# A two-layer float32 trunk on one core: opening, norms' rows, the place of float32 values, and the order of halves' chunks changed

## The chip, the cores and the metric

The kernel runs on one core of one Trainium2 chip. Its time is the device time of one launch in microseconds, the median of three runs. A profile is one further execution, recorded by the hardware profiler. The engines are named as in the profile: PE (TensorE matmul) and PEld (its weight loads), DVE (VectorE), ACT (ScalarE), POOL (GpSimd), SP (SyncE, which issues most transfers).

## What is computed

The reference runs two decoder layers on 256 tokens of width 2048, all in float32. The first layer mixes tokens by softmax attention with a forget gate (16 heads of 128), the second by a mixture of three dilated windows (8 heads, values of 256). Each mixer is followed by an MLP with squared ReLU, and each sub-layer stands behind an RMSNorm and adds into one residual stream.

```python
def rms_norm(x, g):
    y = xf * lax.rsqrt(jnp.mean(xf * xf, axis=-1, keepdims=True) + EPS)
    return (y * g).astype(x.dtype)

def sq_relu_mlp(h, w_up, w_down):
    a = jax.nn.relu(h @ w_up)
    return (a * a) @ w_down

def reference(x, ...):
    for i in range(DEPTH):                      # DEPTH = 2
        h = rms_norm(x, mix_norm_g[i])
        mix = fox_attention(...) if i % 2 == 0 else dilated_attention(...)
        x = x + mix
        h = rms_norm(x, mlp_norm_g[i])
        x = x + sq_relu_mlp(h, mlp_w_up[i], mlp_w_down[i])   # 2048 -> 8192 -> 2048
    return x
```

## The kernel before

**Products.** The whole program is a row of products of 256 tokens with weight matrices that are read once from memory. A weight block of 256 rows and 512 columns (`raw`, 524 KB) is loaded by SP, and split into a high part (`wh`, a cast by ACT) and a low part (`wl`, the difference, by DVE). The activations are split likewise (`hT` for normed inputs, `aTh`/`aTl` for the MLP's inner values, `oT` for attention outputs). A product then takes three matmuls for each 128 rows of the weight (a step, named k) and each of the two token blocks t: high x high, high x low and low x high (lines 421 to 423). One step is therefore six matmuls of 512 columns. A unit is one split weight block, two steps. Five raw blocks and five split units are held at a time, so that loads and splits run ahead of PE; a split of a later unit and the load of a still later one are issued after each unit (`split`, `next_load`, lines 343 and 387).

**Order.** Nothing is left to a scheduler. The program is traced as the main row of products, and every other piece of work (norms, attention heads, gates, the turning of activations) is a generator, a job. After each step the main row calls `jobs.tick()`, which resumes every job whose time has come: `yield 4` in a job means "go on four steps later", `yield key` means "go on when that key is done". The method `pin` fixes that order on each engine. So a number in a `yield` says between which products a piece of work stands in each engine's queue; every engine works through its queue in order.

**Opening.** PE begins with idle matmuls on a tile of zeros (`wake`, line 153). SP loads x in four pieces of 512 columns (`load_x`; the first in three parts), the norm gains and the first weight blocks. The first block comes in two halves (lines 1109 and 1119), the others in one transfer each (line 338). The mixers' norm gains come as rows, `g_mix`, and are turned into columns by a PE transpose and a DVE copy (`gain_rows`, `gain_columns`). For each 128 columns of x PE transposes two blocks into `ptx` (line 564), ACT makes the high part of `hT` and DVE the low one (lines 566 and 567). `row_blocks` splits a unit in halves of 128 rows, so that a step can begin on the first half. The job `opening` issues the first splits, and the job `more_constants` loads the forget gate's weights and two more sets of gains, `g_qk` (8 rows) and `g_mlp` (32 rows), each with a transpose of its own.

**Attention.** A head's scores (`scores`) are one float32 product for the first token block (which the profile shows as two matmuls, a pair) and three split ones for the second. After the softmax its rows are turned through memory (`p_turned`), split (`p_split`, tile pT), and multiplied with the values (`pv`): three split matmuls of 256 columns and one float32 product. `fox_head` and `dil_head` are the jobs of one head; `at` and the yields in them place scores and values. `gate_chain` makes the forget gate's running sums.

**MLP.** Each MLP works on four blocks (b) of 2048 inner columns, each of four chunks (n) of 512. In block 0 all four chunks are plain products. In blocks 1 to 3 the chunks 0 to 2 are made by a Strassen scheme with seven half-sized products for each slice of 256 weight rows (`slice_steps`, tiles halves_n); its weights need sums of quarters (`sum_quarters`), which cost DVE more than a plain unit does. These slices are woven between the units of the down product of block b-1 and of chunk 3 of block b. The lists `BETWEEN` and, for b = 1 (period one), `FIRST_BETWEEN` say after which of the period's 40 units each of the 24 slices (8 for each chunk) stands. A finished chunk goes through `halves_chain` (or `up_chain`, if plain) and `turn_up`: DVE transposes 32x32 squares, SP writes them to memory in four transfers for each token block and reads them back in one, ACT and DVE split the result into `aTh` and `aTl` (lines 1009 and 1011).

Of the kernel before, what the change touches and what calls it, by code (L numbers as in the profile page):

```python
# [46 lines left out]
SUM_TAGS = ("kh3", "kl3", "kh4", "kl4", "kh5", "kl5", "q0", "q1", "q2", "qkw0", "qkw1", "qkw2", "vh", "vl", "pT", "t1")  # L47

BETWEEN = (0, 1, 3, 4, 7, 9, 10, 11, 15, 16, 17, 18, 19, 20, 21, 22, 26, 27, 28, 29, 31, 33, 34, 35)
FIRST_BETWEEN = (0, 1, 2, 6, 8, 9, 10, 11, 15, 16, 17, 19, 20, 21, 22, 23, 27, 28, 30, 31, 33, 34, 36, 37)  # L50


class Jobs:
# [48 lines left out]
def trunk(ctx: ExitStack, tc, x, fox_w_in, fox_b_f, fox_q_gain, fox_k_gain, fox_w_out, dil_w_in,  # L102
# [50 lines left out]
    def wake(times):  # L153
        for _ in range(times):
            nc.tensor.matmul(spare, zeros[:, 0:P], zeros, start=True, stop=True)

    wake(9)


    gain = const.tile([P, 4 * KC + 8], F32, name="gain")  # L160
    MLP_G, FOX_G, DIL_G = 2 * KC, 4 * KC, 4 * KC + 2

    def gain_rows(name, sources):
        rows = work.tile([2 * KC, P], F32, tag="s", name=name, bufs=S_BUFS)
        at = 0
        for src in sources:
            nc.sync.dma_start(rows[at:at + src.shape[0], :], src)
            at += src.shape[0]
        return rows[0:at, :]
# [25 lines left out]
    def more_constants():  # L195
        yield 5
        wf = work.tile([P, KC, FH], F32, tag="t2", name="wf")
        nc.sync.dma_start(wf, fox_w_in[0][:, 3 * D:3 * D + FH].rearrange("(c p) n -> p c n", p=P))
        nc.sync.dma_start(bf, fox_b_f.to_broadcast([P, FH]))
        qk_rows = gain_rows("g_qk", [fox_q_gain, fox_k_gain, dil_q_gain[0], dil_k_gain[0]])  # L200
        mlp_rows = gain_rows("g_mlp", [mlp_norm_g.rearrange(per_chunk, p=P)])
        di = distances()
        yield 9
        nc.scalar.copy(wfs[:, :, 0:FH], wf)
        nc.vector.tensor_sub(wfs[:, :, FH:2 * FH], wf, wfs[:, :, 0:FH].bitcast(F32))
        jobs.done.add("wf")
        yield 1
        gain_columns("g_qk", qk_rows, FOX_G)
        for c in (FOX_G, DIL_G, DIL_G + 1, DIL_G + 2):
            nc.vector.tensor_scalar_mul(gain[:, c:c + 1], gain[:, c:c + 1], SCALE)  # L210
        yield 1
        gain_columns("g_mlp", mlp_rows, MLP_G)
        yield 1
        mask = work.tile([P, 3 * P], F32, tag="t0", name="mask")
        nc.vector.tensor_copy(mask, di)
        nc.vector.tensor_scalar(mask, mask, 0.0, None, ALU.is_ge)
        nc.vector.tensor_scalar(mask, mask, BIG, -BIG, ALU.mult, ALU.add)
        tables["mask"] = mask
        jobs.done.add("mask")
# [108 lines left out]
    def load():  # L328
        i = state["raw"]
        if i >= len(plan):  # L330
            return
        w, r, cols = plan[i]
        t = wpool.tile([P, RAW_SUB, NC], F32, tag="raw", name=f"raw{i}", bufs=RAW_BUFS)
        at = 0
        for c, width in cols:
            src = w[r:r + RAW_SUB * P, c:c + width].rearrange("(c p) n -> p c n", p=P)
            hold(t)
            nc.sync.dma_start(t[:, :, at:at + width], src)
            at += width
        raws.append(t)  # L340
        state["raw"] += 1
# [328 lines left out]
    def by_token(po):  # L670
        return po[:, 0:S].rearrange("p (n b) -> p b n", b=2)

    def pv(pt_sb, vt, cols, o_hi, o_lo, name, apart):
        for i, c in enumerate(cols):
            if i:
                yield 1
            po = ps_sc.tile([P, 512], F32, tag="sc", name=f"po_{name}_{i}")
            whole, v_hi, v_lo = vt
            p_hi, p_lo, p_whole = pt_sb
            for v, p, first in ((v_hi, p_hi, True), (v_hi, p_lo, False), (v_lo, p_hi, False)):  # L680
                nc.tensor.matmul(po[:, 0:S], v[:, c:c + P], p.rearrange("p (b n) -> p n b", b=2), start=first, stop=False)
            nc.tensor.matmul(by_token(po)[:, 1], whole[:, c:c + P], p_whole, start=False, stop=True)
            hi, lo = (o.rearrange("p (b n) -> p b n", b=2) for o in (o_hi[i], o_lo[i]))
            nc.scalar.copy(hi, by_token(po))
            yield apart
            nc.vector.tensor_sub(lo, by_token(po), hi.bitcast(F32))
# [60 lines left out]
    def gate_chain(tag, pf):  # L747
        yield (tag, "rstd")
        tri = work.tile([P, P], F32, tag="s", name="tri", bufs=S_BUFS)
        nc.gpsimd.memset(tri, 1.0)  # L750
        nc.gpsimd.affine_select(out=tri, in_=tri, compare_op=ALU.is_ge, fill=0.0, base=0,
                                pattern=[[1, P]], channel_multiplier=-1)
        ones = work.tile([P, P], F32, tag="s", name="ones", bufs=S_BUFS)
        nc.gpsimd.memset(ones, 1.0)
        f = work.tile([2 * FH, S], F32, tag="s", name="g_f", bufs=S_BUFS)
        nc.vector.tensor_copy(f, pf[:, 0:S])
        nc.vector.tensor_add(f, f, pf[:, S:2 * S])
        yield 3
        pft = ps_sc.tile([P, NT, 2 * FH], F32, tag="sc", name="pft")
        for t in range(NT):  # L760
            nc.tensor.transpose(pft[:, t, :], f[:, t * P:(t + 1) * P], ident[:2 * FH, :2 * FH])
        z = small.tile([P, NT, FH], F32, tag="g_z", name="g_z", bufs=1)
        for t in range(NT):
            r = rstd[tag][:, t:t + 1]
            nc.vector.scalar_tensor_tensor(z[:, t, :], pft[:, t, 0:FH], r, bf, ALU.mult, ALU.add)
            nc.vector.scalar_tensor_tensor(z[:, t, :], pft[:, t, FH:2 * FH], r, z[:, t, :], ALU.mult, ALU.add)

        neg = small.tile([P, NT, FH], F32, tag="g_n", name="g_n", bufs=1)
        nc.vector.tensor_scalar(neg, z, -1.0, None, ALU.mult)
        nc.vector.tensor_tensor(neg, neg, z, ALU.min)  # L770
        e = small.tile([P, NT, FH], F32, tag="g_e", name="g_e", bufs=1)
        nc.scalar.activation(e, neg, AF.Exp)
        yield 1
        u = small.tile([P, NT, FH], F32, tag="g_u", name="g_u", bufs=1)
        nc.vector.tensor_scalar(u, e, 2.0, None, ALU.add)
        nc.vector.reciprocal(u, u)
        nc.vector.tensor_mul(u, e, u)
        u2 = small.tile([P, NT, FH], F32, tag="g_u2", name="g_u2", bufs=1)
        nc.vector.tensor_mul(u2, u, u)
        s = small.tile([P, NT, FH], F32, tag="g_s", name="g_s", bufs=1)  # L780
        nc.vector.tensor_scalar(s, u2, 1.0 / 19.0, None, ALU.mult)
        for odd in (17, 15, 13, 11, 9, 7, 5, 3):
            nc.vector.scalar_tensor_tensor(s, s, 1.0 / odd, u2, ALU.add, ALU.mult)
        nc.vector.scalar_tensor_tensor(s, s, 1.0, u, ALU.add, ALU.mult)
        nc.vector.tensor_scalar(z, z, 0.0, None, ALU.min)
        lf = small.tile([P, NT, FH], F32, tag="g_lf", name="g_lf", bufs=1)
        nc.vector.scalar_tensor_tensor(lf, s, -2.0, z, ALU.mult, ALU.add)
        yield 10
        pc = ps_sc.tile([P, NT, FH], F32, tag="sc", name="pc")
        nc.tensor.matmul(pc[:, 0, :], tri, lf[:, 0, :], start=True, stop=True)  # L790
        nc.tensor.matmul(pc[:, 1, :], ones, lf[:, 0, :], start=True, stop=False)
        nc.tensor.matmul(pc[:, 1, :], tri, lf[:, 1, :], start=False, stop=True)
        nc.vector.tensor_copy(c_q, pc)
        yield 4
        pct = ps_sc.tile([FH, S], F32, tag="sc", name="pct")
        for t in range(NT):
            nc.tensor.transpose(pct[:, t * P:(t + 1) * P], c_q[:, t, :], ident)
        ct = work.tile([FH, 3 * P], F32, tag="s", name="g_ct", bufs=S_BUFS)
        nc.vector.tensor_scalar(ct[:, P:], pct, -1.0, None, ALU.mult)
        nc.vector.tensor_copy(ct[:, 0:P], ct[:, P:2 * P])  # L800
        move(negc, ct)
        jobs.done.add("gate")

    def fox_head(j, hh, qT, kT, vt):
        h = 4 * j + hh
        at = ((2, 7, 12, 16) if j == 3 else (3, 8, 18, 22))[hh]
        yield ("fq", j)
        yield "gate"
        yield "mask"
# [44 lines left out]
    def dil_head(q4, i, qTs, kTs, vt):  # L854
# [30 lines left out]
        turned = yield from p_turned(p, f"d{h}", 6 if q4 == 3 else 10)  # L885
        yield ("dv", q4)
        pt_sb = yield from p_split(turned, f"d{h}")
        yield 2 if q4 == 3 else 4
        if ("d", q4) not in oT:
            oT["d", q4] = tuple(  # L890
                act.tile([P, 4, S], F32R, tag=f"aT{x}", name=f"oTd{x}_{h}", bufs=KC // 4) for x in "hl")
# [234 lines left out]
        what()  # L1126

    gain_columns("g_mix", mix_rows, 0)
    wake(1)
    row_blocks = [slice(i, i + 1) for i in range(W_SUB)]  # L1130
    split(())
    split_part(0, row_blocks[0])
    jobs.spawn(first(0))
    split_part(0, row_blocks[1])
    next_load()
    load_x(3)
    del issued["paced"]
    issued["opening"] = True

    def opening():  # L1140
        yield 1
        split(row_blocks)
        yield 2
        split(row_blocks)
        yield 1
# [73 lines left out]
```

## Time and profile before

| | us |
|---|---|
| median of 3 runs | 2110.7 |
| lowest and highest run | 2109.43, 2110.99 |
| the profiled execution | 2110.77 |
| its span, first to last instruction | 2109.1 |

The page lists for each engine the busy time, its share of the span and the number of instructions; then the chain of work that ended last. A timeline row is: start in us from the span's start, busy us, engine (with q: its sequencer, which issues transfers), line, operation, out<-in by the program's names, shapes, count, and in brackets the idle time of that engine just before, with what ended it. A row of a window has the stretch, its length, the busy us and counts of PE, PEld, DVE, ACT and POOL, the granted clock of PE, the share of the DMA engines and GB/s. A matmul's end is modelled, so the distance between two starts tells more than the shown duration.

### The profile page before, as it was taken

How to read it: one execution, taken by the hardware profiler on the slowest of the kernel's cores; microseconds unless marked ns; L12 is line 12 of the kernel's file. 1: busy time of each engine (PE TensorE's matmuls, PEld its weight loads, DVE VectorE, ACT ScalarE, POOL GpSimd, SP SyncE). 2: the span in 40 equal slices, each digit the busy share in tenths (PEclk: the TensorE clock that was granted, in tenths of full speed). 3: DMA queues.
4: the chain of work that ended last, by engine and by line, in shares of the span. 5: the costliest groups of instructions: out<-in, count | busy, mean ns of one | idle time of the engine just before them, and what ended most of it. 6: DMA issues, size and time to landing. Idle time of an engine off the chain costs nothing.

```text
span 2109.1 us, 32200 instructions
## 1 busy us (share of the span) xinstructions
PE 2100.2 (100%) x11375; PEld 1881.1 (89%) x11375; DVE 1748.1 (83%) x2548; ACT 1288.6 (61%) x1869; POOL 139.9 (7%) x160
## 2 busy tenths in 40 slices
PE   9999999999999999999999999999999999999999
PEld 7888888889998999998888888888899999999988
DVE  6888876799999998988668777767899989999974
ACT  6565654766666666664656565645656666666652
POOL 2000000001001001000010010000001101101100
PEclk9999999999999999999999999999999999999999
DMA  7889877878878878887877776867878878878884
GB/s 244 259 260 266 255 245 215 285 255 230 269 214 250 274 231 251 259 261 244 269 240 228 247 236 213 265 210 242 275 225 251 258 236 251 251 258 245 249 265 150
DMA packets 374993, 518.26 MB, mean 246 GB/s; under 512 B 43096, under 2 KB 176560, under 8 KB 374832
## 3 DMA queue, kind: packets, MB, share of 16 engines
q1 hardware_dynamic: 360592, 503.23, 75.5%
q0 software_dynamic: 13824, 12.59, 3.9%
q8 instruction: 89, 1.46, 0.3%
q10 hardware_dynamic: 416, 0.39, 0.1%
q14 instruction: 72, 0.59, 0.1%
HBM read 463.12 MB, written 40.39 MB: 239 GB/s over the span
## 4 chain that ended last, share of the span: by engine, by line
PE 93%; DVE 3%; ACT 1%; DMA 1%; issue 1%; SPq 0%; ACTq 0%; DVEq 0%
PE acc L422 25%; PE acc L421 25%; PE acc L423 25%; PE halves_n L1061 5%; PE halves_n L1060 5%; PE halves_n L1059 5%; ACT wh L370 1%; DVE wl L371 1%; PE halves_n L1057 0%; DMA raw<-in_dil_w_in_dram 0%; PE sc_d L733 0%; DMA raw<-in_fox_w_in_dram 0%; DVE quarters L380 0%; PE sc_f L733 0%; DMA turned_n1a<-blocks_n1a 0%
## 5 line engine op out<-in xcount | busy, mean ns | idle before, releaser
L371 DVE TENSOR_TENSOR wl<-raw,wh 128x1024 fp32r<-128x1024 f32 (+1 forms) x659 | 790.6, 1213 | 263.4 <-ACT wh L370 254.2
L370 ACT CAST wh<-raw 128x1024 fp32r<-128x1024 f32 (+1 forms) x659 | 680.5, 1043 | 426.6 <-PE acc L423 332.0
L421 PE MATMUL acc<-wh,hT_n 128*128 128x512 f32 x1344 | 512.7, 381 | 1.1 <-ACT wh L370 0.8
L422 PE MATMUL acc<-wl,hT_n 128*128 128x512 f32 x1344 | 509.6, 379 | 0.2 <-DVE wl L371 0.2
L423 PE MATMUL acc<-wh,hT_n 128*128 128x512 f32 x1344 | 509.5, 379 | 0.0
L370 ACT CAST wh<-quarters 128x1024 fp32r<-128x1024 f32 x144 | 151.5, 1052 | 229.7 <-DVE quarters L384 195.0
L423 PEld LDWEIGHTS acc<-wh,hT_n 128*128 128x128 f32 x1344 | 254.0, 189 | 36.2 <-DVE hT_n L567 0.2
L421 PEld LDWEIGHTS acc<-wh,hT_n 128*128 128x128 f32 x1344 | 254.3, 189 | 35.4 <-ACT wh L370 1.2
L422 PEld LDWEIGHTS acc<-wl,hT_n 128*128 128x128 f32 x1344 | 254.3, 189 | 34.4 <-DVE wl L371 0.8
L371 DVE TENSOR_TENSOR wl<-quarters,wh 128x1024 fp32r<-128x1024 f32 x144 | 175.8, 1221 | 36.7 <-ACT wh L370 36.6
L422 PE MATMUL acc<-wl,aTh_n1a 128*128 128x512 f32 x512 | 194.2, 379 | 0.6 <-DVE wl L371 0.6
L421 PE MATMUL acc<-wh,aTh_n1a 128*128 128x512 f32 x512 | 194.2, 379 | 0.0
L423 PE MATMUL acc<-wh,aTl_n1a 128*128 128x512 f32 x512 | 194.0, 379 | 0.0
L422 PE MATMUL acc<-wl,aTh_n3a 128*128 128x512 f32 x480 | 182.0, 379 | 0.6 <-DVE wl L371 0.6
L421 PE MATMUL acc<-wh,aTh_n3a 128*128 128x512 f32 x480 | 182.1, 379 | 0.0
L423 PE MATMUL acc<-wh,aTl_n3a 128*128 128x512 f32 x480 | 181.9, 379 | 0.0
L1061 PE MATMUL halves_n<-wh,sums_n 128*128 128x256 f32 x576 | 158.4, 275 | 0.0
L1060 PE MATMUL halves_n<-wl,sums_n 128*128 128x256 f32 x576 | 158.4, 275 | 0.0
L1059 PE MATMUL halves_n<-wh,sums_n 128*128 128x256 f32 x558 | 153.4, 275 | 0.0
L366 ACT CAST wh<-raw 128x768 fp32r<-128x768 f32 x144 | 119.9, 833 | 53.5 <-PE acc L423 29.3
L368 DVE TENSOR_TENSOR wl<-raw,wh 128x768 fp32r<-128x768 f32 x144 | 137.0, 952 | 2.0 <-ACT wh L366 2.0
L1060 PE MATMUL halves_n<-wl,hT_n 128*128 128x256 f32 x432 | 119.0, 276 | 0.3 <-DVE wl L371 0.3
(664 smaller groups left out, 3374.4 us busy)
## 6 DMA issues: line engine op xcount, KB each, us to landing
raw<-in_mlp_w_up_dram SPq DMA_DIRECT2D x256, 512.0 KB, 5.0
raw<-in_mlp_w_down_dram SPq DMA_DIRECT2D x256, 512.0 KB, 4.9
raw<-in_dil_w_in_dram SPq DMA_DIRECT2D x192, 256.0 KB, 3.5
raw<-in_fox_w_in_dram SPq DMA_DIRECT2D x95, 512.0 KB, 4.9
raw<-in_fox_w_out_dram SPq DMA_DIRECT2D x32, 512.0 KB, 4.8
raw<-in_dil_w_in_dram SPq DMA_DIRECT2D x32, 512.0 KB, 4.6
raw<-in_dil_w_out_dram SPq DMA_DIRECT2D x32, 512.0 KB, 4.3
x<-y_n POOLq DMA_DIRECT2D x96, 128.0 KB, 6.6
```

The costliest lines, as they stand in the source:

```text
L366: nc.scalar.copy(flat_hi, flat)
L368: nc.vector.tensor_sub(flat_lo, flat, flat_hi.bitcast(F32))
L370: nc.scalar.copy(hi[:, part, :], raw[:, part, :])
L371: nc.vector.tensor_sub(lo[:, part, :], raw[:, part, :], hi[:, part, :].bitcast(F32))
L421: nc.tensor.matmul(acc[t], ah[:, tok], hi, start=first, stop=False)
L422: nc.tensor.matmul(acc[t], ah[:, tok], lo, start=False, stop=False)
L423: nc.tensor.matmul(acc[t], al[:, tok], hi, start=False, stop=last)
L1059: nc.tensor.matmul(to, ah, hi, start=pr == 0 and i == 3, stop=False)
L1060: nc.tensor.matmul(to, ah, lo, start=False, stop=False)
L1061: nc.tensor.matmul(to, al, hi, start=False, stop=pr == KC // 2 - 1 and i > 2)
```

## The change

The idle matmuls become 8 (9 + 1 before). The second weight block is loaded in two transfers of 128 rows, and its first half is split before the opening job starts. The gains of `g_qk` and `g_mlp` are gathered in one tile of 40 rows and turned by one transpose; the columns of the gain table move accordingly. In `pv` the float32 product of the values stands third instead of last. One step more is put ahead of the gate's last transposes, of the scores of the first head of the last group of four (j == 3), and of the dilated heads' value products (for the first three groups). In period one 13 of the 24 slices move to earlier units.

```diff
-FIRST_BETWEEN = (0, 1, 2, 6, 8, 9, 10, 11, 15, 16, 17, 19, 20, 21, 22, 23, 27, 28, 30, 31, 33, 34, 36, 37)
+FIRST_BETWEEN = (0, 1, 2, 6, 8, 9, 10, 11, 15, 16, 17, 18, 19, 20, 21, 22, 26, 27, 28, 30, 31, 33, 34, 35)
...
-    wake(9)
+    wake(8)
...
-    MLP_G, FOX_G, DIL_G = 2 * KC, 4 * KC, 4 * KC + 2
+    MLP_G, FOX_G, DIL_G = 2 * KC + 8, 2 * KC, 2 * KC + 2
...
-        rows = work.tile([2 * KC, P], F32, tag="s", name=name, bufs=S_BUFS)
+        rows = work.tile([2 * KC + 8, P], F32, tag="s", name=name, bufs=S_BUFS)
...
-        qk_rows = gain_rows("g_qk", [fox_q_gain, fox_k_gain, dil_q_gain[0], dil_k_gain[0]])
-        mlp_rows = gain_rows("g_mlp", [mlp_norm_g.rearrange(per_chunk, p=P)])
+        rows = gain_rows("g_rest", [fox_q_gain, fox_k_gain, dil_q_gain[0], dil_k_gain[0],
+                                    mlp_norm_g.rearrange(per_chunk, p=P)])
...
-        gain_columns("g_qk", qk_rows, FOX_G)
+        gain_columns("g_rest", rows, FOX_G)
...
-        yield 1
-        gain_columns("g_mlp", mlp_rows, MLP_G)
...
             hold(t)
-            nc.sync.dma_start(t[:, :, at:at + width], src)
+            for rows in [slice(k, k + 1) for k in range(RAW_SUB)] if i == 1 else [slice(0, RAW_SUB)]:
+                nc.sync.dma_start(t[:, rows, at:at + width], src[:, rows])
...
-            for v, p, first in ((v_hi, p_hi, True), (v_hi, p_lo, False), (v_lo, p_hi, False)):
-                nc.tensor.matmul(po[:, 0:S], v[:, c:c + P], p.rearrange("p (b n) -> p n b", b=2), start=first, stop=False)
-            nc.tensor.matmul(by_token(po)[:, 1], whole[:, c:c + P], p_whole, start=False, stop=True)
+            for v, p, at in ((v_hi, p_hi, 0), (v_hi, p_lo, 1), (v_lo, p_hi, 2)):
+                if at == 2:
+                    nc.tensor.matmul(by_token(po)[:, 1], whole[:, c:c + P], p_whole, start=False, stop=False)
+                nc.tensor.matmul(po[:, 0:S], v[:, c:c + P], p.rearrange("p (b n) -> p n b", b=2), start=at == 0, stop=at == 2)
...
         nc.vector.tensor_copy(c_q, pc)
-        yield 4
+        yield 5
...
-        at = ((2, 7, 12, 16) if j == 3 else (3, 8, 18, 22))[hh]
+        at = ((3, 7, 12, 16) if j == 3 else (3, 8, 18, 22))[hh]
...
         pt_sb = yield from p_split(turned, f"d{h}")
-        yield 2 if q4 == 3 else 4
+        yield 2 if q4 == 3 else 5
...
     gain_columns("g_mix", mix_rows, 0)
-    wake(1)
...
     split_part(0, row_blocks[1])
     next_load()
+    split(())
+    split_part(1, row_blocks[0])
     load_x(3)
...
     def opening():
         yield 1
-        split(row_blocks)
+        split_part(1, row_blocks[1])
+        next_load()
         yield 2
```

## The prediction

> **What bounds the kernel now.** I read the page first, then the waits of the tensor engine (PE), then the timelines at the places these waits name.
>
> ```profile
> PE 2100.2 (100%) x11375; PEld 1881.1 (89%) x11375; DVE 1748.1 (83%) x2548; ACT 1288.6 (61%) x1869; POOL 139.9 (7%) x160
> PE 93%; DVE 3%; ACT 1%; DMA 1%; issue 1%; SPq 0%; ACTq 0%; DVEq 0%
> ```
>
> The span is 2109.1 us and PE is busy in all but 9 of them, 93% of the chain that ended last is PE. No edit removes a product, so the change can only give back what PE loses between products. In the waits, a row ends in total us, number of waits, longest:
>
> ```profile
> PE acc L422 <- DVE wl L371: 1.5, 3, 0.6
> ...
> PE po_d L681 <- DVE pT_d L710: 0.3, 1, 0.3
> PE halves_n L1060 <- DVE wl L371: 0.3, 1, 0.3
> PE sc_f L733 <- DVE f_0kl L652: 0.3, 1, 0.3
> ```
>
> These are few, one-off waits, and they understate the loss. A matmul is shown longer than its distance to the next one, so a slip of up to 0.16 shows no idle time. The true price of a wait is read from starts:
>
> ```profile
> 645.50 0.38 PE L421 MATMUL acc<-wh,aTh_n1a 128*128 128x512 f32 x1
> 646.51 0.48 PE L422 MATMUL acc<-wl,aTh_n1a 128*128 128x512 f32 x1 [0.63 <-DVE wl L371]
> 646.83 0.38 PE L423 MATMUL acc<-wh,aTl_n1a 128*128 128x512 f32 x1
> ...
> 33.24 0.38 PE L422 MATMUL acc<-wl,hT_n 128*128 128x512 f32 x1
> 33.45 0.38 PE L423 MATMUL acc<-wh,hT_n 128*128 128x512 f32 x1
> 33.76 0.24 PE L174 MATMUL ps_g_mlp<-ident,g_mlp 32*128 32x32 f32 x1
> 33.94 0.88 PE L744 MATMUL pf<-hT_n,wfs 128*32 128x512 f32 x3
> ```
>
> Undisturbed, a 512-wide matmul follows the last by 0.22 (33.24 to 33.45). At 645.50 the next start is 1.01 away, and the one after that 0.32: 0.79 + 0.10 = 0.89 lost, where 0.63 is shown. So I add 0.27 to each shown wait (0.16 unseen, 0.10 after it).
>
> **The change part by part.**
>
> *Idle matmuls in front (9 to 8, and 1 to 0) and the second load in two.*
>
> ```profile
> 1.52 4.21 PE L155 MATMUL spare<-zeros 128*128 128x512 f32 x9 [1.52 <-DVE zeros L151]
> 5.90 0.80 PE L155 MATMUL spare<-zeros 128*128 128x512 f32 x1
> 6.49 0.67 PE L564 MATMUL ptx_n<-ident,x 128*128 128x128 f32 x4
> 7.51 0.48 PE L421 MATMUL acc<-wh,hT_n 128*128 128x512 f32 x1 [0.35 <-ACT hT_n L566]
> 9.41 0.84 ACT L566 ACTIVATE hT_n<-ptx_n,gain 128x256 fp32r<-128x256 f32 x2 [1.09 <-PE ptx_n L564]
> 11.01 1.14 ACT L370 CAST wh<-raw 128x512 fp32r<-128x512 f32 x2 [0.75 <-DMA raw<-in_fox_w_in_dram]
> 11.68 0.48 PE L421 MATMUL acc<-wh,hT_n 128*128 128x512 f32 x1 [0.79 <-ACT wh L370]
> 13.58 0.60 PE L564 MATMUL ptx_n<-ident,x 128*128 128x128 f32 x4
> 17.31 0.60 PE L564 MATMUL ptx_n<-ident,x 128*128 128x128 f32 x4
> 6.71 1.34 SPq L1114 DMA_DIRECT2D x<-in_x_dram  x1
> DMA to landing us min/median/max: 10.2/10.2/10.2
> ```
>
> ```profile
> 6.70:10.60 3.90, 3.55 (x20) 2.73 (x18) 2.34 (x6) 2.18 (x5) 1.49 (x2) 1.00 0.95 263
> ```
>
> PE sets the time up to 7.51: the ninth idle matmul takes 4.21/9 = 0.47, the tenth 0.59 (5.90 to 6.49). Without them the first product starts about 0.9 to 1.0 earlier. At 11.01 ACT then stands still for the second weight load, and PE for ACT. In two transfers the first half is there sooner: the queues move 263 GB/s here (last column of the window's row), 2.0 us for the load's 524 KB, so half of it is worth about 1.0. Against that, the cast of the first half (1.14/2 = 0.57) now stands ahead of the two hT_n activations (0.42 each) in ACT's queue, and DVE's difference ahead of their low parts. With the half landing near 10.0, PE gets both at 10.0 + 0.57 + 0.42 = 11.0 instead of 11.68, and the transposes at 13.58 would come some 0.7 sooner. But the next ones, at 17.31, read the third piece of x: issued at 6.71, landing 10.2 later, at 16.9. That piece stands in one queue behind the same bytes as before, so it doesn't move. 17.31 - 16.9 = 0.4 is all that survives. Bounds: -0.4 (the half lands no sooner, and ACT stands ahead of hT_n) and +1.0 (the idle matmuls in full, if x too comes sooner). I take 0.4, the landing's row.
>
> *One transpose of the norms' rows.* 33.45 to 33.94 is 0.49, and without the 32-row transpose 0.22: 0.27 saved on PE. The remaining one takes 40 columns instead of 8, some 0.02 more: 0.25. Its rows come by the same five transfers, and the MLP's gains are read only after the output projection. Bounds 0.17 and 0.3.
>
> *Scores and gate moved by a step.*
>
> ```profile
> 289.36 0.38 PE L730 MATMUL sc_f<-f_0w 128*128 128x128 f32 x2
> 290.66 0.38 PE L422 MATMUL acc<-wl,oTfh 128*128 128x512 f32 x1
> ...
> 90.77 0.38 PE L730 MATMUL sc_f<-f_0w 128*128 128x128 f32 x2
> 91.54 0.38 PE L422 MATMUL acc<-wl,hT_n 128*128 128x512 f32 x1
> ...
> 1184.49 0.27 PE L681 MATMUL po_d<-pT_d,dv0h 128*128 128x256 f32 x1
> 1185.87 0.38 PE L422 MATMUL acc<-wl,hT_n 128*128 128x512 f32 x1
> ...
> 118.90 0.39 PE L681 MATMUL po_f<-pT_f,fv0h 128*128 128x256 f32 x2
> 119.68 0.38 PE L422 MATMUL acc<-wl,hT_n 128*128 128x512 f32 x1
> ```
>
> The group of scores takes 0.77 at 90.77 and 1.30 at 289.36: 0.53 lost to f_0kl. The edit at j == 3 puts it one step of the inner loop (six matmuls, 6 x 0.216 = 1.3) later, more than the loss. Its product with the values follows two steps later; its reader is the last part of the output projection, for which heads 13 to 15, placed behind it, are in time too, so nothing waits. The values' group takes 0.78 at 118.90 and 1.38 at 1184.49: 0.60 lost to pT_d, and `yield 5` again gives 1.3. The cast of the next pT_d now waits in ACT's queue for the second group of the head before it, but PE shows no wait for a weight near there. The move of the gate's transposes costs the same on PE in both places: 0. Sum 1.13; bounds 0.5 and 1.13.
>
> *Float32 values third.* The two groups above hold the same work, a float32 pair, three 256-wide and one 512-wide matmul, the one with the pair first, the other with it last: 0.77 and 0.78. So the place of the pair is worth nothing: 0. Bounds:
>
> ```profile
> 119.38 0.46 PE L421 MATMUL acc<-wh,hT_n 128*128 128x512 f32 x1
> ```
>
> From here to 119.68 it is 0.30 instead of 0.22. If those 0.08 are a wait that goes, 32 groups gain 2.6; if one like it is added, they lose 2.6.
>
> *Halves' chunks end sooner in period one.* Four views by window (PE busy follows the length):
>
> ```profile
> 602.00:650.00 48.00, 47.03 (x275) 42.27 (x274) 41.62 (x59) 28.75 (x40) 0.31 (x1) 1.00 0.74 232
> 650.00:810.00 160.00, 160.00 (x982) 147.00 (x981) 147.88 (x203) 104.44 (x145) 14.97 (x19) 1.00 0.83 251
> 810.00:935.00 125.00, 125.00 (x770) 114.93 (x769) 116.16 (x158) 83.75 (x117) 15.22 (x20) 1.00 0.84 253
> 1692.00:1737.00 45.00, 44.37 (x264) 40.24 (x263) 39.18 (x57) 28.03 (x40) 0.31 (x1) 1.00 0.76 237
> ```
>
> At the end of period one of each MLP PE idles 0.97 and 0.63; in periods two and three not at all. What made it so:
>
> ```profile
> 635.50 1.27 ACT L1009 CAST aTh_n1a<-turned_n1a 128x512 fp32r<-128x512 f32 x2 [2.16 <-DMA turned_n1a<-blocks_n1a]
> 637.75 1.22 DVE L371 TENSOR_TENSOR wl<-raw,wh 128x1024 fp32r<-128x1024 f32 x1 [2.78 <-ACT wh L370]
> ```
>
> The last halves chunk and the last plain chunk were turned at once, 16 small writes and 4 reads in SP's queue; ACT waited 2.16 for the reads with the weight casts behind it, DVE 2.78 for ACT, and ten us later PE had used up the lead. With the new list the last two chunks have the places of the later periods' list, save one slice, and the chunk ends two units (5 us) ahead of the plain one. Its turning is then over when the other's begins, as in the two later periods. First MLP: three hits, 0.63 and 0.27 by the waits and 0.07 left of the 0.97, so 0.97 + 3 x 0.27 = 1.78. Second: one hit, 0.63 + 0.27 = 0.90; I leave out what shows no idle time. Gain 2.68. The eight slices that now stand in a row cost DVE some 4.9 us each beside PE's 4.9, as in the later periods. Bounds: 0, if the wait only moves, and 2.8.
>
> Sum: 0.40 + 0.25 + 1.13 + 0 + 2.68 = 4.46. The profiled execution took 2110.77 (span 2109.1 and 1.7 around it), 0.07 over the median of the runs, so 2110.77 - 4.46 = **2106.3**.
>
> **The rivals.**
>
> *The wait stays in the weave.* DVE is 92 to 93% busy in periods two and three too, so there is little to catch up with. If one MLP keeps its hits: 2107.2 or 2108.1; if both do, 2109.0. Against it stand the two later periods without idle time.
>
> *The clock rises late.* The idle matmuls run 0.47 apart, products 0.22, and the change comes near 6.6, five us after the first matmul. With fewer of them and the pause before the first product, the engine may need its five us anew, to 11.7. The first step's six matmuls then take 6 x 0.47 = 2.8 (6.6 to 9.4), four transposes twice their pace, some 0.9, half of the second step is slow, and the third ends at 13.6, no sooner than now. The head's 0.4 is lost: 2106.7. The Trainium skill ("TensorE: Matmul & The Clock Gate", Part 1) says that the clock is doubled after a window of about 3.4 us of sustained activity, and that this window runs free of the kernel's start; by it the rise may come at 10.0 or 13.4, an estimate, and the time would be 2106.3 or some 2107.5. The trace agrees that the first us are at half pace; it can't show where the windows lie.
>
> *Float32 order counts.* If the stretched starts are real and go: 2103.7; if such are added: 2108.9. The equal groups speak against both.
>
> *Slower: ACT waits in four places.* The four aTh casts of chunks two and three no longer stand in pairs, but one by one, each ahead of a weight cast. If two of them wait 2.16 for their reads in each MLP, as one does now, PE loses 2 x 2.16 less the 0.4 of lead that now covers it (2.16 - 1.78): 3.9 in each instead of 1.78 and 0.90. With 1.78 gained elsewhere that is 2110.77 - 1.78 + 2.1 + 3.0 = 2114.1. It decides from 2.2 of lost time on PE in each MLP (4.46 / 2). Later periods have this order, and no such wait.
>
> **How the numbers follow.** The sum 0.66, with its own range 2105.3 to 2107.2 (head -0.4 to +1.0, scores 0.5 to 1.13); the weave's wait stays 0.12; late clock 0.06; float32 gains 0.06, loses 0.05; slower 0.05. A measurement of this kernel can tell about 0.2% from no change, here 4.2 us, so faster means under 2106.5: that line runs through the sum's own range. Faster: 0.45 of the 0.66, and 0.06: 0.51. Same: 0.21 + 0.12 + 0.06 + 0.05 = 0.44. Slower 0.05. The range 2104.6 to 2108.2 holds the sum's case, the late clock and most of one MLP's part of the first rival, some 0.8.
>
> **What would show it.** Right: no wait of PE for wl near 643 to 647 and 1731 to 1733, none for f_0kl near 290 or pT_d near 1185, 100% PE in the end of period one; one transpose of 40 rows near 32; the first product near 6.6; the transposes now at 17.31 at the landing of x's third piece. Wrong: a DMA wait of ACT's aTh casts with PE idle behind it; 512-wide matmuls 0.43 apart after 7; groups of values longer than 0.78; the third piece landing at another time, which moves all that follows by the difference.

## The result, and the profile after

The changed kernel takes 2105.0 us in the median of 12 runs (2104.6 to 2106.8), the kernel before beside it 2110.4 (2109.2 to 2111.4). The ratio is 0.9977, with a 95% interval of 0.9968 to 0.9986; the medians are 5.4 apart. The prediction, 2106.3 with a range of 2104.6 to 2108.2, holds it. The profiled execution took 2104.72, its span is 2103.0.

The page of the changed kernel, engines and the chain that ended last:

```profile
PE 2096.9 (100%) x11372; PEld 1882.4 (90%) x11372; DVE 1748.0 (83%) x2547; ACT 1290.1 (61%) x1869; POOL 139.8 (7%) x160
PE 100%; DVE 0%; ACT 0%; issue 0%
```

The chain is now PE alone, and PE has three matmuls fewer. Its waits (total us, number, longest), all of them:

```profile
PE spare L155 <- DVE zeros L151: 1.5, 1, 1.5
PE acc L420 <- ACT hT_n L565: 0.3, 1, 0.3
```

No wait is left behind the opening: those for wl, for f_0kl and for pT_d are gone. The two windows at the end of period one say the same, with PE busy for their whole length (before 47.03 of 48 and 44.37 of 45):

```profile
602.00:650.00 48.00, 48.00 (x284) 43.80 (x283) 43.46 (x61) 31.27 (x42) 0.00 (x0) 1.00 0.77 253
1692.00:1737.00 45.00, 45.00 (x271) 41.19 (x271) 40.49 (x56) 28.01 (x36) 0.00 (x0) 1.00 0.75 241
6.70:10.60 3.90, 3.90 (x19) 2.79 (x19) 2.69 (x6) 2.58 (x6) 1.95 (x3) 1.00 1.01 362
```

The last of these rows is the opening: the queues moved 362 GB/s from 6.7 to 10.6, where the profiled execution of before moved 263. SP issues x's third piece at 6.39, and it lands 8.3 later, at 14.7 instead of 16.9 (a row of SP's timeline, and the line on the landing of that transfer):

```profile
6.39 0.76 SPq L1114 DMA_DIRECT2D x<-in_x_dram  x1
```

```profile
DMA to landing us min/median/max: 8.3/8.3/8.3
```

PE's timeline at the places of the edits:

```profile
1.52 3.78 PE L155 MATMUL spare<-zeros 128*128 128x512 f32 x8 [1.52 <-DVE zeros L151]
5.47 0.66 PE L563 MATMUL ptx_n<-ident,x 128*128 128x128 f32 x4
6.48 0.48 PE L420 MATMUL acc<-wh,hT_n 128*128 128x512 f32 x1 [0.35 <-ACT hT_n L565]
...
11.35 0.60 PE L563 MATMUL ptx_n<-ident,x 128*128 128x128 f32 x4
...
15.08 0.60 PE L563 MATMUL ptx_n<-ident,x 128*128 128x128 f32 x4
29.88 0.25 PE L174 MATMUL ps_g_rest<-ident,g_rest 40*128 40x40 f32 x1
...
288.14 0.38 PE L730 MATMUL sc_f<-f_0w 128*128 128x128 f32 x2
288.92 0.38 PE L421 MATMUL acc<-wl,oTfh 128*128 128x512 f32 x1
...
1180.98 0.39 PE L682 MATMUL po_d<-pT_d,dv0h 128*128 128x256 f32 x2
1181.75 0.38 PE L421 MATMUL acc<-wl,hT_n 128*128 128x512 f32 x1
...
2098.53 0.28 PE L470 MATMUL last<-wh,aTl_n3a 128*128 128x256 f32 x1
```

Each group of scores or values now takes 0.77 or 0.78 from the first row shown to the last (288.14 to 288.92, 1180.98 to 1181.75), the undisturbed length. The last matmul starts at 2098.53; before it did at 2105.01:

```profile
2105.01 0.28 PE L471 MATMUL last<-wh,aTl_n3a 128*128 128x256 f32 x1
```

I compared the two traces by the start of each product, the n-th with the n-th. The 6.48 between the last matmuls come in six steps and nowhere else: 2.23 in the head (the transposes of x's third piece, 17.31 to 15.08), 0.28 at the norms' transposes, 0.53 at the scores (near 290), 1.77 near 645, 0.61 at the values (near 1185), 1.06 near 1732. Behind the last matmul 0.4 is given back: the span ends 4.5 after it instead of 4.1. That makes the 6.1 between the spans. Where nothing is lost, the products of both kernels keep the same distances.

So between these two executions all terms but one agree with the forecast to 0.2 (0.28 for 0.25, 1.14 for 1.13, 2.83 for 2.68, 0 for the float32 order). The head is worth 2.23 instead of 0.40. And 5.4 between the medians is less than 6.1. The experiments ask what is the edit's and what is the execution's.

### The profile page after: what moved, and what is told of

Read it like the earlier page. It is cut to its first block, busy times and chain, and to the rows that moved or that the text cites. A ratio compares the mean times of both kernels' runs of the same rounds, so it can differ in the third digit from the quotient of the medians.

```text
span 2103.0 us, 32199 instructions
## 1 busy us (share of the span) xinstructions
PE 2096.9 (100%) x11372; PEld 1882.4 (90%) x11372; DVE 1748.0 (83%) x2547; ACT 1290.1 (61%) x1869; POOL 139.8 (7%) x160
## 4 chain that ended last, share of the span: by engine, by line
PE 100%; DVE 0%; ACT 0%; issue 0%
PE acc L420 27%; PE acc L421 27%; PE acc L422 27%; PE halves_n L1061 5%; PE halves_n L1060 5%; PE halves_n L1059 5%; PE halves_n L1057 1%; PE sc_d L733 0%; PE sc_f L733 0%; PE po_f L682 0%; PE po_d L682 0%; PE sc_d L730 0%; PE acc L470 0%; PE acc L468 0%; PE acc L469 0%; PE spare L155 0%
## 5 line engine op out<-in xcount | busy, mean ns | idle before, releaser
L1061 PE MATMUL halves_n<-wh,hT_n 128*128 128x256 f32 x432 | 119.0, 275 | 0.0
```

The source lines that it names most:

```text
L1061: nc.tensor.matmul(to, al, hi, start=False, stop=pr == KC // 2 - 1 and i > 2)
```

## The experiments

Many medians here differ by less than the interval of one ratio (0.0018 wide, some 4 us). So I read two numbers from each trace: the start of the transposes of x's third piece (the head), and from there to the start of the last matmul (the rest).

| kernel | head | last matmul | rest | median of runs | before beside it |
|---|---|---|---|---|---|
| before | 17.31 | 2105.01 | 2087.70 | 2110.39 | |
| before, a second look | 15.78 | 2103.75 | 2087.97 | one run, 2109.52 | 2110.07 |
| before + new slices | 15.97 | 2100.83 | 2084.86 | 2106.67 | 2110.22 |
| before + new opening | 15.36 | 2102.24 | 2086.88 | 2108.92 | 2110.22 |
| changed | 15.08 | 2098.53 | 2083.45 | 2105.02 | 2110.39 |
| changed, values last | 15.31 | 2098.78 | 2083.47 | 2105.10 | 2110.30 |
| changed, steps back | 16.18 | 2100.20 | 2084.02 | 2105.44 | 2110.30 |
| changed, load in one | 15.80 | 2099.26 | 2083.46 | 2105.72 | 2110.22 |
| changed, 9 + 1 idle | 15.61 | 2099.32 | 2083.71 | 2105.25 | 2110.22 |
| changed, 7 idle | 15.32 | 2098.77 | 2083.45 | 2105.88 | 2110.30 |
| changed, 2 idle | 17.18 | 2100.64 | 2083.46 | 2106.35 | 2110.30 |
| changed, old slices | 16.97 | 2103.99 | 2087.02 | 2108.57 | 2110.07 |
| changed, 2nd chunk's new slices | 16.84 | 2103.98 | 2087.14 | 2108.37 | 2110.07 |
| changed, 3rd chunk's new slices | 15.30 | 2098.94 | 2083.64 | 2105.27 | 2110.07 |

The rest is 2083.45 to 2083.47 in five of these traces: without losses it doesn't vary. (With 9 + 1 idle matmuls 0.25 is lost once, at a group of values near 327.) The head does, with the same code.

**Before, a second look.** No edit.

> The kernel before, for a second look at the same instructions: theory A has the transposes of x's third piece at another time than 17.31 (16.0 in the kernel with the new list alone, whose opening is the same), and the losses near 645, 1185 and 1733 of another size than 1.77, 0.61 and 1.06. If theory B is right they are within 0.2 of these.

Its windows, in the opening and at the end of period one:

```profile
6.70:10.60 3.90, 3.81 (x17) 2.66 (x17) 2.91 (x6) 2.81 (x7) 2.20 (x4) 1.00 0.98 361
602.00:650.00 48.00, 46.63 (x273) 41.94 (x272) 40.92 (x58) 28.88 (x41) 0.31 (x1) 1.00 0.74 230
1692.00:1737.00 45.00, 44.16 (x256) 39.77 (x255) 39.84 (x58) 27.72 (x40) 0.00 (x0) 1.00 0.75 236
```

SP's timeline at the issue of x's third piece, the time from this issue to its landing, and PE's timeline:

```profile
5.95 0.93 SPq L1114 DMA_DIRECT2D x<-in_x_dram  x1
```

```profile
DMA to landing us min/median/max: 8.9/8.9/8.9
```

```profile
10.87 0.48 PE L422 MATMUL acc<-wl,hT_n 128*128 128x512 f32 x1 [0.24 <-DVE wl L371]
...
12.05 0.60 PE L564 MATMUL ptx_n<-ident,x 128*128 128x128 f32 x4
...
15.78 0.60 PE L564 MATMUL ptx_n<-ident,x 128*128 128x128 f32 x4
```

The queues move 361 GB/s here too, the third piece lands at 5.95 + 8.9 = 14.85 instead of 16.9, and the head is 1.53 shorter with the same instructions. So of the 2.23, some 1.5 were the execution's and about 0.7 the edit's: the speed of the first transfers is theory A's part. But theory B's part holds as well: the wait for the second block's low part is there again (0.24), and the landing is 0.9 ahead of its use, so it does not bind here. The idle time in the slices is of another size too, 48.00 - 46.63 = 1.37 at the end of the first period one where it was 0.97, and 45.00 - 44.16 = 0.84 at the end of the second where it was 0.63. By the starts the slices lose 3.52 here and 2.83 in the first profile.

**The opening alone, and each half of it taken back.**

The opening's edits, put into the kernel before:

```diff
-    wake(9)
+    wake(8)
...
-            nc.sync.dma_start(t[:, :, at:at + width], src)
+            for rows in [slice(k, k + 1) for k in range(RAW_SUB)] if i == 1 else [slice(0, RAW_SUB)]:
+                nc.sync.dma_start(t[:, rows, at:at + width], src[:, rows])
...
-    wake(1)
...
+    split(())
+    split_part(1, row_blocks[0])
...
-        split(row_blocks)
+        split_part(1, row_blocks[1])
+        next_load()
```

In the changed kernel, the load in one undoes the three hunks of the load and its split, and leaves the idle matmuls; 9 + 1 idle undoes the two hunks with `wake`, and leaves the load.

> The kernel before with the opening's edits alone (8 idle matmuls and none after the gains, second load in two transfers, its first half split ahead). Theory A (as predicted): the landing of x's third piece sets the head's end, so the head is worth 0.4 in the mean, 2110.0 beside a before of 2110.4; the 2.2 between the two profiles at hand comes from a slow start of the transfers in the profiled execution of before (263 GB/s from 6.7 to 10.6 us, 362 in the changed kernel) and is not the edit's. Theory B: the two transfers take PE's wait for the second weight block away whatever the speed, and x's third piece is not what binds: 1.1 to 2.2 gained, 2108.2 to 2109.3. In both, the waits near 290, 643 to 647, 1185 and 1731 to 1733 stay, 4.0 us together.

> The changed kernel with the second load in one transfer again and its split where it was; the idle matmuls stay 8 and 0. Theory A: 0 to 0.4 above the changed kernel (some 2105.0 to 2105.4). Theory B: PE waits for the second block again, about 0.7 for its high part and 0.25 for its low part, and the time is 1.0 to 1.3 above the changed kernel, some 2106.2; the idle matmuls that are gone show as a longer wait there.

> The changed kernel with 9 idle matmuls in front and 1 behind the gains again; the second load stays in two. Theory A: x's third piece sets the end, 0 to 0.4 above the changed kernel. Rival C: the idle matmuls are all on the path, 1.0 above it, some 2106.0, with all of the first three steps 1.0 later and no wait in them shorter.

The opening alone: 2108.9 beside 2110.2, ratio 0.9995 (0.9986 to 1.0004); it lies in theory B's range, but its runs lie between 2107.8 and 2111.1, so this median decides little. Its head is 15.36, where before's is 15.78 to 15.97 when the transfers are quick. With the load in one the head is 15.80, and PE waits for the second block as before, 10.89 - 10.16 = 0.73 between two starts instead of 0.22:

```profile
10.16 0.48 PE L419 MATMUL acc<-wh,hT_n 128*128 128x512 f32 x1
10.89 0.48 PE L420 MATMUL acc<-wl,hT_n 128*128 128x512 f32 x1 [0.24 <-DVE wl L369]
```

With 9 + 1 idle matmuls the head is 15.61 and has no wait for that block at all. The four traces with the changed opening, quick transfers and an early clock have heads of 15.08 to 15.36. So taking back the two transfers costs 0.4 to 0.7 (15.80), and taking back the idle matmuls 0.3 to 0.5 (15.61); both edits together are worth 0.4 to 0.9 (from 15.78 and 15.97). Put in alone, each brings less: the idle matmuls 0 to 0.2 (15.80), since PE then waits for the second block all the same, the two transfers 0.2 to 0.4 (15.61). These are single traces, and the heads of one opening spread by 0.3. The medians, 2105.7 and 2105.3, couldn't tell it; the second is in theory A's range and below rival C's 2106.0.

The landing of the third piece, on which theory A rests, sets the head in none of these traces. Its transposes start 3.73 after those of the second piece (11.35 to 15.08, 12.05 to 15.78, and 13.58 to 17.31 in the first profile of before), and this distance is 3.72 to 3.73 in 13 of the 14 traces, whenever the piece lands. What the edits move is the second piece's transposes.

**Idle matmuls: 7 and 2.** One constant: `wake(7)`, `wake(2)`.

> The changed kernel with 7 idle matmuls instead of 8. If the landing of the second half of the first block and of x's third piece binds: 0 to 0.2 below the changed kernel. If the idle matmuls stand on the path: 0.43 below, 2104.6. If the clock needs them: up to 0.5 above.

> The changed kernel with 2 idle matmuls. PE then does nothing from 2.4 until the first piece of x and the gains land near 4.7. If the clock rises at its own time (5.3 to 6.7 in the six traces so far), whatever PE has done: the first product at 6.0 to 6.5 and a time within 0.5 of the changed kernel. If it needs some 3.8 to 5.1 us of work before it (the six traces' distance from the first matmul, 1.52): it rises between 8.5 and 9.9, the first two steps run at half pace, and the time is 1 to 2 above, 2106 to 2107.

Seven: the head is 15.32, no better than with eight; nothing is left to gain there. The median is 0.86 above the changed kernel's, more than the 0.5 that was expected at most, and six of the ten runs are at 2105.8 to 2106.6; the profile is of a quick one (2104.95), so what they lost isn't seen. Two, PE's timeline:

```profile
1.52 1.22 PE L155 MATMUL spare<-zeros 128*128 128x512 f32 x2 [1.52 <-DVE zeros L151]
5.07 0.28 PE L174 MATMUL ps_g_mix<-ident,g_mix 32*128 32x32 f32 x1 [2.32 <-POOL x L321]
...
6.54 0.80 PE L420 MATMUL acc<-wh,hT_n 128*128 128x512 f32 x1
7.12 0.63 PE L421 MATMUL acc<-wl,hT_n 128*128 128x512 f32 x1
7.55 0.63 PE L422 MATMUL acc<-wh,hT_n 128*128 128x512 f32 x1
...
11.39 0.50 PE L420 MATMUL acc<-wh,hT_n 128*128 128x512 f32 x1
11.73 0.38 PE L421 MATMUL acc<-wl,hT_n 128*128 128x512 f32 x1
11.94 0.38 PE L422 MATMUL acc<-wh,hT_n 128*128 128x512 f32 x1
```

The first product starts at its usual time, but the matmuls stand 0.43 apart (7.12 to 7.55) until about 11.4, then 0.21. The head is 17.18, 2.1 later than in the changed kernel. The clock rises later than even the second theory said (8.5 to 9.9). One such trace can't show that the missing idle matmuls are the cause, since the clock rose late in two traces with eight as well (below). The runs speak for it: with two idle matmuls 9 of 11 take 2106.0 or more, with eight 3 of 12, with 9 + 1 none of 10.

**The slices.** The new list put into the kernel before, and the old one into the changed kernel:

> The kernel before with the new list of slices in period one alone. As predicted: 2.7 gained (2.8 by the starts of the matmuls in the changed kernel's trace), 2107.6 to 2107.7 beside a before of 2110.4, with no wait of PE near 643 to 647 and 1731 to 1733. Rival: the list needs the later yields too, and a wait of 0.5 or more for wl stays in one MLP. Its head is the one of before: theory A says that the third piece of x lands anywhere between 14.6 and 16.9 in it, theory B that PE stands 0.7 or more for the second block in any execution.

> The changed kernel with the old list of slices in period one. As predicted: the three hits near 643 to 647 less the shift and the one near 1733 come back, 2.7 to 2.8 above the changed kernel, 2107.8. Since the new list alone gained 3.55 in the medians and 2.8 by the starts in the trace, a second theory: the loss differs from execution to execution and is some 3.5 in the median, 2108.5, with runs spread over more than 1.5, while the kernels with the new list have a tail of 2083.45 behind the transposes of x's third piece in every trace.

The kernel before with the new list, by window:

```profile
602.00:650.00 48.00, 48.00 (x280) 43.63 (x279) 43.35 (x63) 30.41 (x41) 0.31 (x1) 1.00 0.81 258
```

It takes 2106.67 beside 2110.22 (ratio 0.9984, 0.9975 to 0.9992), 3.55 gained; there is no wait for wl near 645 or 1732, and its rest differs from the lossless 2083.45 by 1.41 only: 0.28, 0.53 and 0.6 at the values. With the old list 2108.57, 3.55 above the changed kernel; its rest is 3.57 above 2083.45, and no other edit is undone. The other three traces with the old list lose 2.83, 3.52 and 2.58 in the slices (their rest, less 2083.45 and what the scores, values and transposes lose), and the runs with it spread over 3.0 (2107.1 to 2110.2). So the worth of the new list lies there, and it differs from execution to execution, as the second theory said.

PE's timeline of this last kernel held something else, in its opening, which is the changed one:

```profile
5.47 1.11 PE L563 MATMUL ptx_n<-ident,x 128*128 128x128 f32 x4
6.72 0.80 PE L420 MATMUL acc<-wh,hT_n 128*128 128x512 f32 x1
7.31 0.63 PE L421 MATMUL acc<-wl,hT_n 128*128 128x512 f32 x1
7.74 0.63 PE L422 MATMUL acc<-wh,hT_n 128*128 128x512 f32 x1
...
10.73 0.51 PE L421 MATMUL acc<-wl,hT_n 128*128 128x512 f32 x1
11.08 0.38 PE L422 MATMUL acc<-wh,hT_n 128*128 128x512 f32 x1
...
16.97 0.60 PE L563 MATMUL ptx_n<-ident,x 128*128 128x128 f32 x4
```

Eight idle matmuls stood in front, and yet the four transposes take 1.11 instead of 0.66 and the products run 0.43 apart until 11: the clock rose late, as with two. The head is 16.97, 1.6 to 1.9 later than where it rose early. One more kernel was profiled in such an execution, the one with the second chunk's new slices (head 16.84).

**Which of the slices.** The new list differs in two parts, the eight slices of the second chunk, of which five moved, and the eight of the third, which all moved.

With the third chunk's eight:

```diff
-FIRST_BETWEEN = (0, 1, 2, 6, 8, 9, 10, 11, 15, 16, 17, 18, 19, 20, 21, 22, 26, 27, 28, 30, 31, 33, 34, 35)
+FIRST_BETWEEN = (0, 1, 2, 6, 8, 9, 10, 11, 15, 16, 17, 19, 20, 21, 22, 23, 26, 27, 28, 30, 31, 33, 34, 35)
```

With the second chunk's eight:

```diff
-FIRST_BETWEEN = (0, 1, 2, 6, 8, 9, 10, 11, 15, 16, 17, 18, 19, 20, 21, 22, 26, 27, 28, 30, 31, 33, 34, 35)
+FIRST_BETWEEN = (0, 1, 2, 6, 8, 9, 10, 11, 15, 16, 17, 18, 19, 20, 21, 22, 27, 28, 30, 31, 33, 34, 36, 37)
```

> The changed kernel, but of the new list of slices only the last eight (the third halves chunk); the second chunk's eight stand as before. Theory T (as predicted: the third halves chunk and the plain one are turned at once): these eight take the whole loss away, 2105.0 to 2105.2, 2083.5 behind the transposes of x's third piece. Rival S (the slices of both chunks take PE's lead): about half comes back, 2106.4.

> The converse: of the new list only the second chunk's eight, the last eight as before. Theory T: the loss of the old list in full, 2107.8 to 2108.5, with ACT waiting for the turned reload near 632 to 636 and PE for wl some ten us later. Rival S: about half of it, 2106.4.

The third chunk's eight do it all: 2105.27 and a rest of 2083.64 (0.2 of which is lost near 557). With the second chunk's eight the loss is there in full, 2108.37 and 2087.14. Theory T holds against S. In that kernel ACT's casts of the turned blocks, and PE behind them:

```profile
634.92 1.31 ACT L1009 CAST aTh_n1a<-turned_n1a 128x512 fp32r<-128x512 f32 x2 [2.84 <-DMA turned_n1a<-blocks_n1a]
637.82 1.13 ACT L1009 CAST aTh_n1a<-turned_n1a 128x512 fp32r<-128x512 f32 x2
```

```profile
642.08 0.38 PE L1060 MATMUL halves_n<-wl,hT_n 128*128 128x256 f32 x1 [0.80 <-DVE wl L367]
...
645.97 0.48 PE L421 MATMUL acc<-wl,aTh_n1a 128*128 128x512 f32 x1 [0.63 <-DVE wl L370]
```

And the same casts with the third chunk's eight:

```profile
625.64 0.63 ACT L1009 CAST aTh_n1a<-turned_n1a 128x512 fp32r<-128x512 f32 x1 [2.16 <-DMA turned_n1a<-blocks_n1a]
628.29 0.62 ACT L1009 CAST aTh_n1a<-turned_n1a 128x512 fp32r<-128x512 f32 x1
632.00 0.62 ACT L1009 CAST aTh_n1a<-turned_n1a 128x512 fp32r<-128x512 f32 x1 [2.12 <-DMA turned_n1a<-blocks_n1a]
634.20 0.61 ACT L1009 CAST aTh_n1a<-turned_n1a 128x512 fp32r<-128x512 f32 x1
```

ACT waits for the reads here too, and longer in sum (2.16 + 2.12 against 2.84). But each cast stands alone, with weight casts between, over nine us instead of four, and PE loses nothing.

**Values and steps.**

The float32 product last again:

```diff
-            for v, p, at in ((v_hi, p_hi, 0), (v_hi, p_lo, 1), (v_lo, p_hi, 2)):
-                if at == 2:
-                    nc.tensor.matmul(by_token(po)[:, 1], whole[:, c:c + P], p_whole, start=False, stop=False)
...
+            for v, p, first in ((v_hi, p_hi, True), (v_hi, p_lo, False), (v_lo, p_hi, False)):
...
+            nc.tensor.matmul(by_token(po)[:, 1], whole[:, c:c + P], p_whole, start=False, stop=True)
```

And the three steps back:

```diff
-        yield 5
+        yield 4
...
-        at = ((3, 7, 12, 16) if j == 3 else (3, 8, 18, 22))[hh]
+        at = ((2, 7, 12, 16) if j == 3 else (3, 8, 18, 22))[hh]
...
-        yield 2 if q4 == 3 else 5
+        yield 2 if q4 == 3 else 4
```

> The changed kernel with the float32 product of the values last again. As predicted (the place of the pair is worth nothing): the groups of values take 0.77 to 0.78 as before, and the time is that of the changed kernel, 2105.0, within 0.5. Rival: 32 groups stretched by 0.08 each, 2.6 above, 2107.6; or, if the third place is the worse one, 2102.4. Its opening is the changed kernel's, so its profile is a further look at that head: theory A has x's third piece land at another time than 14.6, theory B has PE reach the transposes of that piece at 15.1 again.

> The changed kernel with the three steps taken back (4 ahead of the gate's transposes, 2 for the first head of the last group, 4 ahead of the dilated values). As predicted: 1.1 above the changed kernel, 2106.1 to 2106.2, with a loss of 0.53 on f_0kl near 287 and 0.6 on pT_d near 1180. Rival: the new slices or the float32 product in third place have already moved these, and less than 0.5 comes back.

Values last: the rest is 2083.47, the changed kernel's to 0.02 over 32 groups. The place of the pair is worth nothing. The steps back: the scores lose their 0.53 again, the rest is 2084.02 and so 0.57 above 2083.45, half of the 1.1 that was expected. PE's timeline at the scores, and its transposes in the opening:

```profile
288.12 0.36 PE L733 MATMUL sc_f<-f_0kh,f_0q 128*128 128x256 f32 x1
288.75 0.38 PE L733 MATMUL sc_f<-f_0kl,f_0q 128*128 128x256 f32 x1 [0.27 <-DVE f_0kl L651]
...
12.12 0.63 PE L563 MATMUL ptx_n<-ident,x 128*128 128x128 f32 x4 [0.45 <-DMA x<-in_x_dram]
16.18 0.63 PE L563 MATMUL ptx_n<-ident,x 128*128 128x128 f32 x4
```

At the values nothing comes back. The 0.61 near 1185 is a matter of the execution: with the value products at their old place the traces lose 0.6 (before), 0.2 (second look), 0.6 (new slices), 0 (new opening) and 0 here; with the new place 0 in all nine traces. So the step is worth 0.3 in the mean of these five, but the three that lose all have before's opening; that it helps in the changed kernel isn't shown. The last two rows are an execution of the changed opening with slow transfers (250 GB/s from 6.7 to 10.6). PE does wait for x's second piece (0.45 shown at 12.12), and the third lands at 16.05; here its transposes come 4.06 behind those of the second, 0.13 after the landing. It is the one trace in which this landing sets the head.

## Why the prediction was right, and where a term was off

*The head, 0.40.* The step that failed is "17.31 - 16.9 = 0.4 is all that survives": it took the landing of x's third piece for what ends the head. That holds in one trace with slow transfers; in the 13 others the distance of 3.72 to 3.73 from the second piece's transposes sets it. The first profile of before is such a slow execution (263 GB/s), and there the cap would have held: with the transposes at 13.58 only 0.7 sooner, the third piece, at 16.9, comes last. In before's two other traces it lands at 14.9 and 15.0, 0.9 ahead of its use, and the edit takes 0.4 to 0.9, about 0.6 in the mean, without reaching the landing. The 2.23 between the two profiles, beyond the bound of +1.0, is this and the luck of the one execution, 1.5 (17.31 to 15.78).

*One transpose of the rows, 0.25.* Measured 0.28.

*Scores and values, 0.53 + 0.60.* The scores gave 0.53, and undoing the step gave it back, to 0.04. The 0.60 at the values was one execution's loss; the five traces lose 0 to 0.6, about 0.3 in the mean. A wait seen once was counted as a constant. The bound of 0.5 covered it.

*Float32 third, 0.* Shown by the trace with the old order; the two equal groups were enough to say so.

*The slices, 2.68.* 2.83 between the profiles, 2.6 to 3.6 over the four traces with the old list, 3.55 in the medians of both kernels that have one list and the other's surroundings. The edit was right and the size somewhat low, again because the loss varies and one execution was read. The mechanism is half right: the eight slices of the third chunk are the cause, but "its turning is then over when the other's begins" is not what the trace shows. ACT still waits for the reads, 2.3 in all in the changed kernel's window from 600 to 650; the waits now come apart, with weight casts between. That the spacing and not the earlier time (625 for 635) keeps PE supplied is argued from these rows; no run changed one without the other.

*The rivals.* That the weave's wait stays, and that the order of the float32 product counts, are refuted above. The slower case, ACT waiting for its reads in several places, did come about in the kernel with the third chunk's new slices alone: 2.16 and 2.12 in one MLP, as large as the price assumed. It cost PE nothing, so its price was wrong and not its event. The late clock is the rival that partly happened. In two of the eight traces with eight idle matmuls the clock rose near 11, and the head is 1.5 to 1.9 later, not 0.4: the rival was priced against the slow head of 17.31, and 16.97 and 16.84 are indeed near it. These two executions were the slowest of their kernels' runs (2110.15 and 2110.13). Of the changed kernel's 12 runs three are at 2106.5 to 2106.8, the others at 2104.6 to 2105.6, a gap of the same size; that these three are late clocks is likely, but they weren't profiled, and slow first transfers, which cost the first profile of before 1.5, would look the same. With 9 + 1 idle matmuls 21 runs of two kernels lie within 0.7 (2104.9 to 2105.6, and 2106.6 to 2107.1). So the removed idle matmuls gain 0.3 to 0.5 when the clock rises in time and seem to lose 1.7 in about a quarter of the executions: next to nothing in the mean. The mean of the changed kernel's 12 runs is 2105.35, that of the 10 runs with 9 + 1 is 2105.24.

*What would beat both.* The rest of the changed kernel shows no loss that is left to take away, and in the quick executions with an early clock its head ends 0.1 to 0.5 behind the landing. The version with 9 + 1 idle matmuls is as quick in the mean and spreads by 0.6 instead of 2.2; a difference in the median to the changed kernel can't be shown.

*The sum.* The edit's part by these runs is 0.4 to 0.9 + 0.28 + 0.53 + 0.3 + 2.6 to 3.6 = 4.1 to 5.6, where 4.46 was forecast and 5.4 was measured. The 2105.0 lies in the stated range, but below the sum's own range of 2105.3 to 2107.2: head and slices were both taken somewhat low.

## What to carry to other kernels

Take a second profile of the same kernel before pricing a wait: of this kernel's five losses two were constant to 0.05 (scores, transposes), and three changed by 0.6 to 1.5 from execution to execution. Where several helper casts share a queue with the casts that feed PE, look at how they are spaced before looking at how long they wait. Idle matmuls in front seem to buy not only an early clock but a safe one; their worth shows in the spread of the runs, not in the median.

## What the runs showed of the hardware

When PE's clock rises differs from execution to execution. After eight idle matmuls it rose between 5.5 and 6.7 us in six traces and near 11 in two, with the same instructions up to there in most of them. After two and a pause of 2.3 us it rose 6.3 us after PE resumed (5.07 to 11.4), in the one trace of it.

The Trainium skill ("TensorE: Matmul & The Clock Gate", Part 1) says that the clock is raised after a busy window of about 3.4 us, and that these windows run free of the kernel. PE works from 1.52 on, so by that the rise is due between 4.9 and 8.3, an estimate from the page's figure; the early rises agree, the late ones, near 11, don't. PE pauses by no more than 0.14 before the first product in them (5.47 + 1.11 = 6.58, and 6.72), and no run shows where the windows lie.

The first transfers differ from execution to execution. With before's opening they moved 263 GB/s in one profile and 354 and 361 in two others over the same 3.9 us, and the third piece of x landed at 16.9, 15.0 and 14.9. With the changed opening it was 250 in one profile and 324 to 362 in the others. And the last output transfer ended the span 4.0 to 4.1 after the last matmul in six traces and 4.4 to 4.5 in the other eight.
